# Rotary embedding over sixteen batches: the first store is issued by GpSimd instead of ScalarE

## The chip, the cores and the metric

The kernel runs on one core of one Trainium2 chip. A core has five instruction streams: TensorE (matmuls), VectorE (DVE), ScalarE (ACT), GpSimd (POOL) and SyncE (SP). Each stream executes in order, and waits on semaphores that the others and the DMAs raise. Data moves between the chip's main memory (DRAM) and the core's on-chip memory by DMA; sixteen DMA engines do the moving, and a DMA is put to them by an instruction on SyncE, ScalarE or GpSimd. Each of these issuers has a queue of its own. The metric is the device time of one execution, in microseconds (us); lower is better.

## The reference: what is computed

The input `x` is 16 batches of 512 positions of 1024 numbers (f32); the 1024 numbers are 16 heads of 64. In each head the first 32 numbers (`x1`) and the last 32 (`x2`) are rotated by an angle that depends on the position alone:

```python
x = x.reshape(batch, seq, num_heads, head_dim)
x1, x2 = x[..., :half_dim], x[..., half_dim:]
rotated = np.concatenate([
    x1 * cos - x2 * sin,
    x1 * sin + x2 * cos
], axis=-1)
```

`cos` and `sin` are 512 by 32. Input and output are 33.55 MB each, so 67.1 MB pass through the DMA engines in every execution.

## The kernel before

**Tiling.** The work is cut into eight slabs. A slab is 128 partitions by 8192 f32 numbers, which is 32 KB in each partition and 4.19 MB in all. An on-chip buffer called `room` has six slots of one slab each (`slots = 6`), and slab s lives in slot s modulo 6. Loading, computing and storing all work in place in the slot.

**Loads** (line 71, on SyncE). Six DMAs bring the eight slabs: slabs 0 and 1 singly, slabs 2 and 3 as one DMA of 8.39 MB, slabs 4 and 5 as one of 8.39 MB, and slabs 6 and 7 singly (the dictionary `loads`). The first four are issued at the start. Slab 6 goes into the slot of slab 0, so its load may be issued only once the store of slab 0 has landed; slab 7 waits in the same way for the store of slab 1.

**Compute.** A slab of the middle of the kernel is one pass; slabs 0, 6 and 7 are two passes of half a slab each. A pass has five instructions:

- ScalarE casts the f32 data to bf16 in place (line 144, "the cast");
- VectorE multiplies twice with the cos and sin tables (line 165) and adds (line 168), all in bf16;
- ScalarE writes the result back as f32 over the slot (line 170, "the widening").

The tables themselves are built once at the start, by GpSimd, TensorE and VectorE (lines 79 to 133).

**Stores** (line 174, on ScalarE). Seven DMAs: slabs 0, 1, 2 and 3 singly, slabs 4 and 5 together (8.39 MB), slabs 6 and 7 singly. Because they are issued by ScalarE, a store's instruction stands in the same in-order stream as the casts and widenings.

**What sets the order.** The source is a plain loop over the passes, but the framework under it reorders the instructions of each engine with its own estimates of durations, and so the order on ScalarE is not exactly that of the source. In the kernel before, the order on ScalarE around the first stores is: cast of slab 0 (two halves), cast of slab 1, widening of slab 0 (two halves), store of slab 0, cast of slab 2, widening of slab 1, cast of slab 3, store of slab 1, widening of slab 2, cast of slab 4, store of slab 2, widening of slab 3, cast of slab 5, store of slab 3, widening of slab 4, first cast of slab 6, widening of slab 5, second cast of slab 6, store of slabs 4 and 5. A store's issue starts about 0.1 us after the instruction ahead of it has started, if the widening that it needs is done.

The functions that the change touches:

Of the kernel before, what the change touches and what calls it, by code (L numbers as in the profile page):

```python
# [2 lines left out]

# [4 lines left out]


@with_exitstack  # L10
def kernel(
    ctx: ExitStack,
    tc: tile.TileContext,
    x: bass.AP,
    cos: bass.AP,
    sin: bass.AP,
    num_heads: int,
    out: bass.AP,
):
    nc = tc.nc  # L20
    P = nc.NUM_PARTITIONS

    batch, seq, dim = x.shape
    nh = num_heads
    hd = dim // nh
    half = hd // 2
    bf16 = mybir.dt.bfloat16
    f32 = mybir.dt.float32

    nb = 2  # L30
    slots = 6
    nslabs = batch // nb
    G = 2
    rpp = nb * seq // P
    W = rpp * dim
    SP = seq // rpp
    TW = rpp * half

    out_flat = out.rearrange("b s h d -> b s (h d)")

    singles = ctx.enter_context(tc.tile_pool(name="singles", bufs=1))
    psum = ctx.enter_context(tc.tile_pool(
        name="psum", bufs=1, space=bass.MemoryType.PSUM))


    def dram(t, s, k):
        return bass.AP(tensor=t.tensor,
                       offset=t.offset + s // G * (G * nb * seq * dim) + s % G * W,
                       ap=[[G * W, P], [1, k * W]])


    def view(t, offset, *dims):
        return dataclasses.replace(t, offset=t.offset + offset,
                                   ap=[t.ap[0], *[list(d) for d in dims]])


    room = singles.tile([P, slots * W], f32, tag="room")
    halves = room.bitcast(bf16)


    def slab(s, k):
        return view(room, s % slots * W, (1, k * W))


    loads = {0: 1, 1: 1, 2: 2, 4: 2, 6: 1, 7: 1}
    stores = {0: 1, 1: 1, 2: 1, 3: 1, 4: 2, 6: 1, 7: 1}


    def load(s):
        k = loads[s]  # L70
        nc.sync.dma_start(out=slab(s, k), in_=dram(x, s, k))  # L71

    TR = 32
    TQ = seq // TR // rpp
    TC = seq * half // TR
    raw = singles.tile([P, TC], f32, tag="raw")
    nc.vector.memset(raw, 0.0)  # L79


    def load_tables(queue):
        for i, src in enumerate((cos, sin)):
            to = dataclasses.replace(
                raw, offset=raw.offset + i * raw.ap[0][0],
                ap=[[P // TR * raw.ap[0][0], TR], [1, TC]])
            queue.dma_start(out=to, in_=bass.AP(
                tensor=src.tensor, offset=src.offset, ap=[[TC, TR], [1, TC]]))


    load(0)
    load_tables(nc.scalar)
    for s in loads:
        if 0 < s < slots:
            load(s)

    GP = SP // G
    GT = G // TQ  # L100
    pick = singles.tile([P, 3 * GT * P], bf16, tag="pick")
    nc.gpsimd.memset(pick, 0.0)  # L102


    def selection(g, h):
        return pick[:, (g * GT + h // TQ) * P:(g * GT + h // TQ + 1) * P]


    for g in range(3):
        for h in range(0, G, TQ):  # L110
            part = view(selection(g, h), 0, (GP, P // GP), (1, GP))
            nc.gpsimd.affine_select(  # L112
                out=part, in_=part, compare_op=mybir.AluOpType.not_equal,
                fill=-1.0 if g == 2 else 1.0,
                base=-(1 if g else 0) - h // TQ * (P // TR),
                pattern=[[0, P // GP], [-(G // TQ) * (P // TR), GP]],
                channel_multiplier=1)

    raw_b = singles.tile([P, TC], bf16, tag="raw_b")
    nc.gpsimd.tensor_copy(out=raw_b, in_=raw)  # L120

    tab = {}


    def table(h):
        acc = psum.tile([P, 2 * rpp * hd], f32, tag=f"acc{h}")
        for g, at in ((0, 0), (0, half), (2, rpp * hd), (1, rpp * hd + half)):
            nc.tensor.matmul(  # L128
                view(acc, at, (hd, rpp), (1, half)), selection(g, h),
                view(raw_b, h % TQ * TW, (half, rpp), (1, half)),  # L130
                start=True, stop=True)
        tab[h] = singles.tile([P, 2 * rpp * hd], bf16, tag=f"tab{h}", name="tab")
        nc.vector.tensor_copy(out=tab[h], in_=acc)  # L133

    def span(u):
        s, r, n = u
        at, m = s % slots * W + r * dim, n * dim
        return (m, view(room, at, (1, m)), view(halves, 2 * at, (1, m)),
                view(halves, 2 * at + m, (1, m)))


    def cast(u):
        m, full, low, high = span(u)
        nc.scalar.copy(out=low, in_=full)  # L144

    passes = []
    for s in range(nslabs):  # L150
        n = rpp if 1 <= s < nslabs - 2 else rpp // 2
        passes += [(s, r, n) for r in range(0, rpp, n)]


    cast(passes[0])
    for i, u in enumerate(passes):
        s, r, n = u
        if s < G and r == 0:
            table(s)
        if i + 1 < len(passes):  # L160
            cast(passes[i + 1])
        m, full, low, high = span(u)
        turned = view(low, half, (hd, n * nh), (-half, 2), (1, half))
        for out_, in_, a in ((high, turned, rpp * hd), (low, low, 0)):
            nc.vector.tensor_mul(  # L165
                out=out_, in0=in_,
                in1=view(tab[s % G], a + r * hd, (hd, n), (0, nh), (1, hd)))
        nc.vector.tensor_add(out=high, in0=low, in1=high)  # L168

        nc.scalar.copy(out=full, in_=high)  # L170
        if r + n == rpp:
            for t, k in stores.items():
                if t + k - 1 == s:
                    nc.scalar.dma_start(out=dram(out_flat, t, k), in_=slab(t, k))  # L174
                    for v in range(t + slots, t + k + slots):
                        if v in loads:
                            load(v)


# [1 line left out]
_INS = ['x', 'cos', 'sin', 'num_heads']  # L181
_OUTS = [((16, 512, 16, 64), 'float32')]

_NUMBERS = {'num_heads': 16}


# [26 lines left out]
```

## Time and profile before

| what | us |
|---|---|
| median of 3 runs | 162.26 (162.25 to 162.39) |
| the profiled execution's own time | 162.28 |
| its span in the profile | 160.5 |
| VectorE busy | 109.9 (68% of the span) |
| ScalarE busy | 113.3 (71%) |
| GpSimd busy | 2.1 (1%) |
| share of 16 DMA engines' span, both queues together | 98.0% |

In the profile, instructions are named by engine and by line of the kernel (L144 is the cast). `ACTq`, `SPq` and `POOLq` are the issuing sides of ScalarE, SyncE and GpSimd. A DMA's issue takes some tenths of a microsecond; the time from there until the data have landed is given apart. `q1` is SyncE's DMA queue and `q10` is ScalarE's (the loads and the stores, told apart by their bytes). A packet of the DMA is one row of one partition: 32,768 bytes for a DMA of one slab, 65,536 for a DMA of two.

### The profile page before, as it was taken

The numbers are of one execution on the slowest core, as the hardware profiler recorded it, in microseconds if no ns is written. First come the engines' busy times: TensorE is split into PE (matmuls) and PEld (weight loads), VectorE is DVE, ScalarE is ACT, GpSimd is POOL, SyncE is SP. The second block draws the span as 40 slices with busy tenths as digits, with TensorE's granted clock in tenths as the row PEclk, the third lists the DMA queues.
The fourth block names the chain that finished last, engine by engine and source line by source line (L and its number), as shares of the span: only waits on it lengthen the run. The fifth ranks groups of instructions, "written<-read, shape, count | busy, mean of one in ns | idle before, by whom it ended". The sixth has DMA issues, their size and how long they took to land.

```text
span 160.5 us, 162 instructions
## 1 busy us (share of the span) xinstructions
PE 1.9 (1%) x8; PEld 1.1 (1%) x8; DVE 109.9 (68%) x36; ACT 113.3 (71%) x23; POOL 2.1 (1%) x9
## 2 busy tenths in 40 slices
PE   0004000000000000000000000000000000000000
PEld 0002000000000000000000000000000000000000
DVE  1002999999900999899789989999649999800000
ACT  3006939991089999997999999929999999170000
POOL 3001000000000000000000000000000000000000
DMA  7999999969599999999999999999996996999994
GB/s 261 408 408 392 523 392 523 506 278 523 245 408 392 555 490 392 392 392 392 465 441 400 433 474 400 433 474 400 408 604 294 523 490 294 400 474 433 392 474 180
DMA packets 1968, 67.24 MB, mean 419 GB/s; under 512 B 240, under 2 KB 240, under 8 KB 304
## 3 DMA queue, kind: packets, MB, share of 16 engines
q1 hardware_dynamic: 864, 33.55, 49.4%
q10 hardware_dynamic: 1104, 33.69, 48.6%
HBM read 33.69 MB, written 33.55 MB: 419 GB/s over the span
## 4 chain that ended last, share of the span: by engine, by line
ACT 36%; DMA 27%; DVE 13%; issue 12%; another core or an unknown queue 1%; SPq 0%; ACTq 0%
DMA room<-in_x_dram 27%; ACT room L170 22%; ACT room L144 14%; DVE room L165 8%; DVE room L168 4%; SPq L71 0%; ACTq L174 0%; ACTq L170 0%
## 5 line engine op out<-in xcount | busy, mean ns | idle before, releaser
L165 DVE TENSOR_TENSOR room<-room,tab 128x4096 bf16<-128x4096 bf16 (+1 forms) x22 | 71.6, 3259 | 15.0 <-ACT room L144 14.6
L144 ACT CAST room<-room 128x4096 bf16<-128x4096 f32 (+1 forms) x11 | 56.6, 5153 | 20.9 <-DMA room<-in_x_dram 20.9
L170 ACT CAST room<-room 128x4096 f32<-128x4096 bf16 (+1 forms) x11 | 56.6, 5154 | 6.6 <-DVE room L168 6.6
L168 DVE TENSOR_TENSOR room<-room 128x4096 bf16<-128x4096 bf16 (+1 forms) x11 | 35.9, 3261 | 0.3
L133 DVE CAST tab<-acc 128x1024 bf16<-128x1024 f32 x2 | 2.4, 1219 | 13.6 <-PE acc L128 13.6
L144 ACT ACT_TABLE_LOAD x1 | 1.3, 1283 | 2.7 <-issue 2.7
L128 PE MATMUL acc<-raw_b,pick 128*128 128x256 bf16 x8 | 1.9, 415 | 13.9 <-POOL raw_b L120 13.9
L128 PEld LDWEIGHTS <-pick 128*128 128x128 bf16 x8 | 1.1, 140 | 14.2 <-issue 12.2
L79 DVE MEMSET raw<- 128x512 f32 x1 | 0.5, 485 | 0.9 <-PEq L194 0.9
L112 POOL TENSOR_SCALAR_AFFINE_SELECT pick<-pick 128x128 bf16<-128x128 bf16 x3 | 0.8, 309 | 0.1
L120 POOL CAST raw_b<-raw 128x512 bf16<-128x512 f32 x1 | 0.6, 610 | 11.2 <-DMA raw<-in_sin_dram 11.2
L102 POOL MEMSET pick<- 128x384 bf16 x1 | 0.4, 418 | 0.3 <-POOLq L194 0.3
L194 POOL MEMSET const-float32-0.0<- 128x1 f32 x1 | 0.1, 98 | 0.2 <-issue 0.2
L194 POOL MEMSET const-bfloat16-1.0<- 128x1 bf16 x1 | 0.1, 101 | 0.0
L194 POOL MEMSET const-uint8-127<- 128x1 uint8 x1 | 0.1, 101 | 0.0
L194 POOL MEMSET const-float32-1.0<- 128x1 f32 x1 | 0.1, 98 | 0.0
## 6 DMA issues: line engine op xcount, KB each, us to landing
out_dram<-room ACTq DMA_DIRECT2D x6, 4096.0 KB, 32.5
room<-in_x_dram SPq DMA_DIRECT2D x4, 4096.0 KB, 22.3
raw<-in_cos_dram ACTq DMA_DIRECT2D x1, 64.0 KB, 7.9
raw<-in_sin_dram ACTq DMA_DIRECT2D x1, 64.0 KB, 11.1
room<-in_x_dram SPq DMA_DIRECT2D x2, 57.5
out_dram<-room ACTq DMA_DIRECT2D x1, 25.1
```

Source lines behind the costliest of these rows:

```text
L79: nc.vector.memset(raw, 0.0)
L102: nc.gpsimd.memset(pick, 0.0)
L112: nc.gpsimd.affine_select(out=part, in_=part, compare_op=mybir.AluOpType.not_equal, fill=-1.0 if g == 2 else 1.0, base=-(1 if g else 0) - ...
L120: nc.gpsimd.tensor_copy(out=raw_b, in_=raw)
L128: nc.tensor.matmul(view(acc, at, (hd, rpp), (1, half)), selection(g, h), view(raw_b, h % TQ * TW, (half, rpp), (1, half)), start=True, sto ...
L133: nc.vector.tensor_copy(out=tab[h], in_=acc)
L144: nc.scalar.copy(out=low, in_=full)
L165: nc.vector.tensor_mul(out=out_, in0=in_, in1=view(tab[s % G], a + r * hd, (hd, n), (0, nh), (1, hd)))
L168: nc.vector.tensor_add(out=high, in0=low, in1=high)
L170: nc.scalar.copy(out=full, in_=high)
L194: nc = _bacc.Bacc("TRN2", target_bir_lowering=False, num_devices=1)
```

## The change

[...]

```diff
         if r + n == rpp:
             for t, k in stores.items():
                 if t + k - 1 == s:
-                    nc.scalar.dma_start(out=dram(out_flat, t, k), in_=slab(t, k))
+                    queue = nc.scalar if t else nc.gpsimd
+                    queue.dma_start(out=dram(out_flat, t, k), in_=slab(t, k))
```

The built program differs in more than this one instruction, because the framework orders ScalarE's stream anew. The start of it, from the widening of slab 0 on (line 174 of before is line 175 of after):

```
before                         after
widening slab 0 (two halves)   widening slab 0 (two halves)
store slab 0                   widening slab 1
cast slab 2                    cast slab 2
widening slab 1                store slab 1
cast slab 3                    cast slab 3
store slab 1                   widening slab 2
widening slab 2                cast slab 4
cast slab 4                    store slab 2
...                            ...
```

From the widening of slab 2 on, the two orders are the same. On GpSimd the new store is the last instruction of the stream; it waits for the widening of slab 0's second half. VectorE's order and SyncE's order of instructions do not change; the load of slab 6 waits for GpSimd's store of slab 0, and the load of slab 7 for ScalarE's store of slab 1.

## The prediction

> **What bounds the kernel now.** I read the page's busy line first and the DMA lines under it, then DMA by stretches, then the order in time with the waits.
>
> ```profile
> PE 1.9 (1%) x8; PEld 1.1 (1%) x8; DVE 109.9 (68%) x36; ACT 113.3 (71%) x23; POOL 2.1 (1%) x9
> DMA packets 1968, 67.24 MB, mean 419 GB/s; under 512 B 240, under 2 KB 240, under 8 KB 304
> q1 hardware_dynamic: 864, 33.55, 49.4%
> q10 hardware_dynamic: 1104, 33.69, 48.6%
> ```
>
> No compute engine is over 71% busy; the DMA engines are taken for 98.0% of the span. 67.24 MB at the 434 GB/s that the undisturbed stretches move are 155 us of the 160.5. So little can be gained: the first packets' delay, the last landing, and one dip below. Much can be lost, if the DMA engines are ever left without work.
>
> The DMA view between 46 and 68 us, and between 36 and 44 us, when the first store starts:
>
> ```profile
> DMA packets 192, 9.44 MB, mean 429 GB/s; under 512 B 0, under 2 KB 0, under 8 KB 0
> q1 hardware_dynamic: 96, 6.29, 65.9%
> q10 hardware_dynamic: 96, 3.15, 33.1%
> ...
> DMA packets 66, 2.92 MB, mean 365 GB/s; under 512 B 9, under 2 KB 9, under 8 KB 9
> ```
>
> Between 46 and 68, loads (q1) and store 0 (q10) have equal numbers of packets, 96 and 96: the queues take turns. A load packet of 64 KB takes 2.42 us on its engine, a store packet of 32 KB 1.21, so a round is 3.63 us. Between 36 and 44, (429 - 365) / 429 of 8 us is lost: a dip of 1.2 us, in which the packet that runs as the first store starts takes 3.6 to 3.9 us instead of 2.42 (single packets are read from the trace).
>
> Order in time:
>
> ```profile
> 36.93 0.35 ACTq L174 DMA_DIRECT2D out_dram<-room  x1
> 39.62 4.42 DVE L168 TENSOR_TENSOR room<-room 128x8192 bf16<-128x8192 bf16 x1
> 44.91 7.02 ACT L144 CAST room<-room 128x8192 bf16<-128x8192 f32 x1 [8.02 <-DMA room<-in_x_dram]
> 51.84 7.01 ACT L170 CAST room<-room 128x8192 f32<-128x8192 bf16 x1
> 51.96 8.89 DVE L165 TENSOR_TENSOR room<-room,tab 128x8192 bf16<-128x8192 bf16 x2 [7.92 <-ACT room L144]
> 58.88 0.34 ACTq L174 DMA_DIRECT2D out_dram<-room  x1
> 65.68 7.01 ACT L170 CAST room<-room 128x8192 f32<-128x8192 bf16 x1
> 73.80 7.02 ACT L144 CAST room<-room 128x8192 bf16<-128x8192 f32 x1 [1.11 <-DMA room<-in_x_dram]
> 115.17 0.34 ACTq L174 DMA_DIRECT2D out_dram<-room  x1
> ...
> SPq L71 <- DMA out_dram<-room: 87.4, 2, 67.3
> ```
>
> ScalarE stands idle from 36.9 to 44.9 for slabs 2 and 3, and slab 1's widening, whose sum is ready at 39.62 + 4.42 = 44.04, stands behind that cast. Slab 4's cast waits for its load until 73.8. The last line is SyncE holding the loads of slabs 6 and 7 for stores 0 and 1.
>
> DMA issued from ScalarE in 87-89, 114-116, 128-131 and 142-145, with the time to landing:
>
> ```profile
> out_dram<-room ACTq DMA_DIRECT2D x1, 4096.0 KB, 33.2
> ...
> out_dram<-room ACTq DMA_DIRECT2D x1, 25.1
> ...
> out_dram<-room ACTq DMA_DIRECT2D x1, 4096.0 KB, 20.6
> ...
> out_dram<-room ACTq DMA_DIRECT2D x1, 4096.0 KB, 16.1
> ```
>
> Issue plus landing: store 3 lands at 87.77 + 33.2 = 120.95, stores 4/5 at 140.3, 6 at 150.0, 7 at 159.6. The steps, 19.3, 9.7 and 9.7, are exactly the bytes at 434 GB/s, so at the end each store queues behind the one before. The cover of compute over DMA is smallest at stores 4/5: issued at 115.17, while store 3 lands at 120.95. If that issue slips by more than the cover, DMA stands still and the end moves.
>
> **The change, part by part.** The sum is made against the profiled execution: span 160.5, time 162.28, 1.8 around it, against a median of 162.26.
>
> *Issue taken from ScalarE (0.35 us).* It falls in ScalarE's idle 8 us: worth nothing. Without that cover it would be 0.35.
>
> *Issue added on GpSimd.* GpSimd's stream is empty after its table cast at 13.9 us and nothing is queued behind the store: no cost there. [...]
>
> *ScalarE's new order.* Widening of slab 1 now starts at 44.06, and the cast of slab 2 one pitch of a full slab later (51.84 - 44.91 = 6.93), at 51.0 instead of 44.91. Store 1 is issued at 51.1 instead of 58.88. Cast of slab 3 at 57.9. VectorE does slab 2 in 13.34 us (51.96 to 65.30 before), now 58.0 to 71.35; the widening of slab 2 starts at 71.4 (before 65.68), and the cast of slab 4 can start at 78.35 instead of 73.80. This 4.55 us is certain if the order is kept.
>
> *The third queue.* Store 0 has GpSimd's queue, store 1 comes into ScalarE's at 51.1 and no longer stands behind it. If the queues still take turns, a round is 2.42 + 1.21 + 1.21. Load 4/5 has 8.39 MB / 16 / 65,536 = 8 packets on each engine, of which 6 start after 52; in 5 to 6 of those rounds store 1 adds a packet of 1.21, 6.1 to 7.3 us. Load 4/5, landed at 73.78 before, lands at 79.9 to 81.1, and that, not 78.35, starts the cast of slab 4. Stores 0 to 2 and loads 6 and 7 gain or lose nothing by it: the same bytes in another order. Store 0 lands near 73, load 6 after 23.7 us as before is there before its cast is due (it started at 101.49 before, 27.7 after that of slab 4).
>
> *The end.* From the cast of slab 4 to the issue of stores 4/5 is 115.17 - 73.80 = 41.4 us in either order; now 121.3 to 122.5. The DMA engines run out of work where store 3 landed, 120.95, since the bytes ahead are the same. What a start on idle engines costs, the first load bounds: 12.6 us to landing less 9.7 of transfer is 2.9; the tables' packets take 0.3 of it, and the very first packets, at 1.9 instead of 1.2, 0.7. I take 1.9, between 1.6 (the first packet 1.0 after the first issue, the last landing 0.6 after its packet) and 2.9. The end moves by (cast of slab 4) + 41.4 + 1.9 - 120.95, that is by that cast's start less 77.65: 2.25 to 3.45, middle 2.85. Stores 6 and 7, issued 55.5 and 69.7 after the cast, come before the DMA needs them.
>
> *The dip.* 1.2 us, gone or kept: no row shows a GpSimd store. I keep it, since the next queue's first store may pay it as well.
>
> Sum: 0 + 0 + 2.85 = 2.85; 162.28 + 2.85 = 165.1.
>
> **Rivals.**
>
> *A: turns longer or shorter than a row.* The rows show one row per turn for the two queues there are. If GpSimd's queue gave its 8 rows per engine in one turn, that is 9.7 us in which loads 2/3 cannot end: from 44.9 to about 53.4, the cast of slab 2 at 53.4 instead of 51.0, slab 4's at 80.8 to 82.5: 3.2 to 4.85 more, 166.3. [...] With turns much smaller than a row, store 0 gets its bytes mostly after load 4/5 (about 70) and shares with store 1 or 2 from there: 4.19 MB at 217 GB/s, landing near 90 to 92. Load 6, 20.6 to 23.7 later at 113, holds the cast in front of slab 5's widening; stores 4/5 go out at 113 + 3.5 + 6.9 = 123.4, plus 4.4: 166.7.
>
> *B: store 0 starts late.* VectorE works from 35.16 to 44.04 without a gap. If GpSimd's descriptors had to wait for it, store 0 would start 7 us late, one or two of its packets would fall behind load 4/5, and slab 4's cast would be at 78.35 to 79.9: 0.7 to 2.25, about 163.8. [...] No run here shows it.
>
> *C, the other side: the dip goes.* If GpSimd's start does not disturb the running packet, 1.2 us come back at 40 us and everything behind moves up with it. It ends faster only if load 4/5 is in by 78.35 as well, with at most three packets of store 1 ahead of its end (73.78 - 1.2 + 3 x 1.21 = 76.2): 0.7 - 1.2 = -0.5, 161.8, at best 161.1 if the start on idle engines were nothing to pay. For it: the dip is there once, at a first store of ScalarE. Against: store 1 has 20 us beside load 4/5. With the dip gone and the turns as forecast it is 163.9.
>
> **How the numbers follow.** Forecast 0.45 (165.1, its own range 164.5 to 165.7). A 0.20 (166.3 to 166.7). B 0.12 (163.8). C with late loads 0.09 (163.9). C with loads in time 0.14 (161.1 to 162.3). Within 0.2%, some 0.3 us, is what a measurement here cannot tell from no change: the edges of B and C make 0.08; faster 0.12; slower 0.80. The range leaves out most of C's fast end and the worst of A: 161.9 to 167.0.
>
> **What would show it.** Right: store 1 issued at 51, cast of slab 2 at 51, cast of slab 4 at 80 to 81 with a wait for DMA, stores 4/5 issued near 122, a hole in the DMA there, three queues with packets between 53 and 73. Wrong: slab 4's cast at 78.4 with no wait; store 0 landing near 50 or 90; loads 2/3 late; no dip at 40 us; or a hole elsewhere.

## The result, and the profile after

The changed kernel takes 164.38 us (median of 5 runs, 164.0 to 165.18) where the kernel before takes 162.25 (now of 5 runs as well, 162.06 to 162.39): 1.0133 times as long, with a 95% interval of 1.012 to 1.0147. Forecast were 165.1 us, slower with a chance of 0.80, and a range of 161.9 to 167.0. The profiled execution took 164.26, with a span of 162.5 against 160.5.

The page of the changed kernel, the DMA line, the line of each queue (packets, MB, share of 16 engines' span) and the group of the new store:

```profile
DMA packets 1968, 67.24 MB, mean 414 GB/s; under 512 B 240, under 2 KB 240, under 8 KB 304
q1 hardware_dynamic: 864, 33.55, 48.9%
q10 hardware_dynamic: 960, 29.49, 42.1%
q0 software_dynamic: 144, 4.19, 6.0%
L175 POOL DMA_DIRECT2D out_dram<-room x1 | 0.7, 690 | 23.3 <-ACT room L170 23.3
```

The bytes and packets are the same; the 4.19 MB of store 0, issued by GpSimd, are in a third queue, `q0`. The profile gives its kind as software_dynamic, that of the other two as hardware_dynamic; it is called the software ring below, and what stands behind the name no run shows. Share by share, 97.0% of the DMA engines' time is taken instead of 98.0%, in a longer span: 1% of 160 us have become idle, and the packets' own time is unchanged. So the loss is DMA engines without work, and the question is only where.

The changed kernel in order of time, the lines that answer to those shown of before:

```profile
37.20 0.69 POOL L175 DMA_DIRECT2D out_dram<-room  x1 [23.32 <-ACT room L170]
39.63 4.43 DVE L168 TENSOR_TENSOR room<-room 128x8192 bf16<-128x8192 bf16 x1
44.15 7.02 ACT L170 CAST room<-room 128x8192 f32<-128x8192 bf16 x1 [7.24 <-DVE room L168]
51.07 7.01 ACT L144 CAST room<-room 128x8192 bf16<-128x8192 f32 x1
51.19 0.35 ACTq L175 DMA_DIRECT2D out_dram<-room  x1
71.55 7.02 ACT L170 CAST room<-room 128x8192 f32<-128x8192 bf16 x1 [6.54 <-DVE room L168]
79.94 7.02 ACT L144 CAST room<-room 128x8192 bf16<-128x8192 f32 x1 [1.37 <-DMA room<-in_x_dram]
121.31 0.34 ACTq L175 DMA_DIRECT2D out_dram<-room  x1
```

Slab 1's widening now runs from 44.15, before the cast of slab 2, which slips from 44.91 to 51.07. Store 1 goes out at 51.19 instead of 58.88. The widening of slab 2 starts at 71.55 and ends at 78.6, and then ScalarE waits 1.37 for load 4/5: its cast of slab 4 starts at 79.94 instead of 73.80, and everything behind it on ScalarE is 6.1 late, up to the issue of stores 4/5 at 121.31 instead of 115.17.

The DMA view of the changed kernel between 54 and 70 us, the queues' lines:

```profile
q1 hardware_dynamic: 48, 3.15, 45.4%
q10 hardware_dynamic: 64, 2.10, 30.3%
q0 software_dynamic: 48, 1.57, 22.8%
```

These are the turns of three queues: three load packets (2.42 us each on its engine), three of store 0 and four of store 1 (1.21 each) on every engine, the fourth by where the cut falls. Loads had 65.9% of the DMA engines while store 0 alone stood beside them; now they have 45.4%, and load 4/5 lands at 79.92 instead of 73.78.

In the single packets, every engine moves one row of the load, one of store 1 and one of store 0 by turns, from 55 to 71 us.

The stretches of the changed kernel around the issue of stores 4/5 (us, then busy time and count of PE, PEld, DVE, ACT and POOL, clock, DMA share and GB/s; a packet counts whole where it starts):

```profile
119.00:120.00 1.00, 0.00 (x0) 0.00 (x0) 1.00 (x1) 1.00 (x1) 0.00 (x0) 1.00 0.76 328
120.00:121.00 1.00, 0.00 (x0) 0.00 (x0) 1.00 (x1) 1.00 (x1) 0.00 (x0) 1.00 0.01 0
121.00:122.00 1.00, 0.00 (x0) 0.00 (x0) 0.03 (x1) 1.00 (x2) 0.00 (x0) 1.00 0.00 0
122.00:123.00 1.00, 0.00 (x0) 0.00 (x0) 0.00 (x0) 1.00 (x1) 0.00 (x0) 1.00 2.46 1049
```

No packet of a row starts between 120 and 122 (the 0.01 is packets of 4 bytes). Store 3's last packets, of 1.21 us, end at 120.0 to 120.6 and the first of stores 4/5 start at 122.1 to 122.3: each engine stands still for 1.6 to 2.3 us, 1.9 on average. In the kernel before, all sixteen engines have started on stores 4/5 by 120.6, without a gap behind store 3. Its stretches from 120 to 122:

```profile
120.00:121.00 1.00, 0.00 (x0) 0.00 (x0) 0.97 (x1) 1.00 (x1) 0.00 (x0) 1.00 2.12 918
121.00:122.00 1.00, 0.00 (x0) 0.00 (x0) 0.99 (x1) 1.00 (x1) 0.00 (x0) 1.00 0.00 0
```

The zero in its second row is no idle time: the packets that started between 120 and 121 take 2.42 us each.

The landing of the four last DMAs of ScalarE in the changed kernel, cut out as the four were for the kernel before:

```profile
out_dram<-room ACTq DMA_DIRECT2D x1, 4096.0 KB, 27.1
...
out_dram<-room ACTq DMA_DIRECT2D x1, 20.8
...
out_dram<-room ACTq DMA_DIRECT2D x1, 4096.0 KB, 16.3
...
out_dram<-room ACTq DMA_DIRECT2D x1, 4096.0 KB, 11.8
```

Store 3 lands at 93.91 + 27.1 = 121.0, as before (120.95). Stores 4/5 land at 121.31 + 20.8 = 142.1, which is 1.8 later than before, store 6 at 151.8 and store 7 at 161.5, 1.9 later than before. Up to 120 us nothing is lost, and behind 122 next to nothing more: the program ends 1.0 us after the last landing, where it was 0.9 in the kernel before.

### The profile page after: what moved, and what is told of

Read it like the earlier page. It is cut to its first block, busy times and chain, and to the rows that moved or that the text cites. A ratio compares the mean times of both kernels' runs of the same rounds, so it can differ in the third digit from the quotient of the medians.

```text
span 162.5 us, 166 instructions
## 1 busy us (share of the span) xinstructions
PE 1.9 (1%) x8; PEld 1.1 (1%) x8; DVE 109.8 (68%) x36; ACT 113.3 (70%) x23; POOL 2.7 (2%) x10
## 3 DMA queue, kind: packets, MB, share of 16 engines
q0 software_dynamic: 144, 4.19, 6.0%
## 4 chain that ended last, share of the span: by engine, by line
DVE 37%; ACT 37%; issue 8%; DMA 7%; another core or an unknown queue 1%; PE 1%; ACTq 1%; POOL 0%; POOLq 0%; DVEq 0%
DVE room L165 25%; ACT room L170 24%; ACT room L144 13%; DVE room L168 11%; DMA raw<-in_sin_dram 7%; DVE tab L133 1%; PE acc L128 1%; POOL raw_b L120 0%; ACTq L87 0%; DVE raw L79 0%; ACTq L175 0%; ACTq L170 0%; POOLq L120 0%; DVEq L165 0%
## 5 line engine op out<-in xcount | busy, mean ns | idle before, releaser
L165 DVE TENSOR_TENSOR room<-room,tab 128x4096 bf16<-128x4096 bf16 (+1 forms) x22 | 71.6, 3259 | 21.3 <-ACT room L144 20.8
L175 POOL DMA_DIRECT2D out_dram<-room x1 | 0.7, 690 | 23.3 <-ACT room L170 23.3
## 6 DMA issues: line engine op xcount, KB each, us to landing
out_dram<-room ACTq DMA_DIRECT2D x1, 20.8
```

The costliest lines, as they stand in the source:

```text
L165: nc.vector.tensor_mul(out=out_, in0=in_, in1=view(tab[s % G], a + r * hd, (hd, n), (0, nh), (1, hd)))
L175: queue.dma_start(out=dram(out_flat, t, k), in_=slab(t, k))
```

## The experiments

The forecast's rule, with the idle start as the changed kernel shows it: stores 4/5 are issued 41.4 after the cast of slab 4 starts; on idle DMA engines they land 1.47 later than their transfer of 19.33 takes (142.11 - 121.31 - 19.33); store 3 has landed at 120.95. So the end moves by the start of slab 4's cast less 78.1, and not at all below that. The 1.47 is the changed kernel's own, so the other runs test the rule and the changed kernel does not. Each run is compared with runs of the kernel before on the same chip.

**The order alone.** Store 0 stays with ScalarE; slab 1's widening goes ahead of slab 2's cast.

```diff
-        if i + 1 < len(passes):
+        if i + 1 < len(passes) and s != 1:
             cast(passes[i + 1])
...
-        nc.scalar.copy(out=full, in_=high)
+        wide = nc.scalar.copy(out=full, in_=high)
+        if s == 1:
+            with tc.issue_after(wide.ins):
+                cast(passes[i + 1])
```

> The change's new order on ScalarE without its queue: store 0 stays with ScalarE, issued right behind slab 0's widening as before, and slab 1's widening goes ahead of slab 2's cast as in the changed kernel. Theory (the end moves by the start of slab 4's cast plus 41.4 to the issue of stores 4/5, plus 1.5 to start idle DMA engines, less the 120.95 at which store 3 lands): load 4/5 lands near 73.8 as before, slab 4's cast starts at 78.35 because of the order, stores 4/5 go out at 119.7, the end moves by 0.2, time 162.3 to 162.6. Rival, the order alone costs all of it: 164.2 to 164.5. Rival, the software ring costs all of it: 162.25, and no sign of an order's effect.

Measured: 162.65 against 162.31, ratio 1.0021 (1.0011 to 1.003); that is 0.05 above the theory's range. In its order of time the cast of slab 4 stands without a wait for DMA:

```profile
78.36 7.01 ACT L144 CAST room<-room 128x8192 bf16<-128x8192 f32 x1
```

Load 4/5 landed at 73.81 and store 1, though issued at 51.08, behind store 0 at 90.7, as in the kernel before. The rule gives 78.36 - 78.1 = 0.26 for the 0.34 measured. The order alone is one sixth of the loss.

**The queue alone.** Store 0 is issued by GpSimd; ScalarE's order is held to that of before.

```diff
-            cast(passes[i + 1])
+            nxt = cast(passes[i + 1])
...
-        nc.scalar.copy(out=full, in_=high)
+        if s == 1:
+            with tc.issue_after(nxt.ins):
+                nc.scalar.copy(out=full, in_=high)
+        else:
+            nc.scalar.copy(out=full, in_=high)
```

> The change's queue without its new order: store 0 is issued by GpSimd, and ScalarE's order is held to that of before (slab 2's cast ahead of slab 1's widening), so store 1 goes out at 58.9. Theory: three queues take turns only from 59 on, load 4/5 lands at 77.4 to 78.8 instead of 79.9, slab 4's cast starts there, stores 4/5 go out at 118.8 to 120.2, just inside or just outside the cover: time 162.2 to 162.9. Rival, the software ring itself is what costs: 164.2 to 164.5. Rival, only the order matters: 162.25.

Measured: 162.41 against 162.31, ratio 1.0004 (0.9995 to 1.0014): no change that can be measured. Yet the third queue does its work on load 4/5, which lands at 77.52, and on the cast that waits for it:

```profile
77.54 7.02 ACT L144 CAST room<-room 128x8192 bf16<-128x8192 f32 x1 [4.78 <-DMA room<-in_x_dram]
```

ScalarE waits 4.78 instead of 1.11, and it costs nothing, because 77.54 is still under 78.1. So the software ring as such is not the cost. The two parts alone come to 0.44 us; together they cost 2.1. Both draw on the same cover, but they do not simply add. Here load 4/5 lands three packets of 1.21 us later than before; in the changed kernel it is five, because the new order also issues store 1 at 51.19 instead of 58.95, and so store 1 stands beside the load for longer. ScalarE is free for slab 4's cast at 78.57 in the changed kernel, and it is the load that holds the cast until 79.94.

**Store 1 in the software ring too.** ScalarE's order is written out as in the changed kernel, so that no third queue arises beside load 4/5; VectorE's order is left to the framework.

```diff
-        queue = nc.scalar if t else nc.gpsimd
+        queue = nc.scalar if t > 1 else nc.gpsimd
```

> The changed kernel with store 1 moved to GpSimd as well, behind store 0 in the same software ring; ScalarE's order is written out and is that of the changed kernel. Theory: there is no third queue beside the loads while load 4/5 is under way, so load 4/5 lands near 73.8, slab 4's cast starts at 78.35, the end moves by 0.2: 162.3 to 162.7, though twice the bytes go through the software ring. Rival, each store in the software ring costs by itself: 166 or more. Rival, the loss is that of the order: 164.4.

Measured: 167.12 against 162.31, ratio 1.0294 (1.0279 to 1.031). The number is one that the first rival allows (166 or more), and far from the theory's. But load 4/5 landed at 73.62, as the theory says, and the cast of slab 4 was at 82.77 all the same. The order of time shows why: the framework had given VectorE one of slab 3's multiplications ahead of slab 2's addition.

```profile
58.19 13.22 DVE L186 TENSOR_TENSOR room<-room,tab 128x8192 bf16<-128x8192 bf16 x3 [14.06 <-ACT room L144]
71.33 4.42 DVE L189 TENSOR_TENSOR room<-room 128x8192 bf16<-128x8192 bf16 x1
75.84 7.02 ACT L190 CAST room<-room 128x8192 f32<-128x8192 bf16 x1 [10.76 <-DVE room L189]
```

Slab 2's addition starts at 71.33, its widening at 75.84 instead of 71.55. Three multiplications stand in the row where the changed kernel has two. The rule gives 82.77 - 78.1 = 4.7; measured 4.8.

**The same with VectorE's order written out.**

```diff
+            with tc.issue_after(added) if s > 1 else nullcontext():
                 nc.vector.tensor_mul(
...
-        nc.vector.tensor_add(out=high, in0=low, in1=high)
+        added = nc.vector.tensor_add(out=high, in0=low, in1=high).ins
```

> The run with stores 0 and 1 both in the software ring, once more, with VectorE's order written out as well: there, VectorE had been given a multiplication of slab 3 ahead of the addition of slab 2, which put slab 4's cast at 82.8. Theory: load 4/5 lands near 73.7 again, slab 4's cast starts at 78.4, stores 4/5 go out at 119.8, the end moves by 0.2 to 0.4 and the time is 162.4 to 162.8. Rival, two stores in the software ring cost more than one: 165 to 167 with slab 4's cast at 78.4.

Measured: 162.97 against 162.28, ratio 1.0068 (1.0034 to 1.0103); the medians alone are 0.4% apart. The median is 0.2 above the theory's range. Of ten executions seven took 162.8 to 163.0, and three 164.7 to 165.9. The seven are far from 165 to 167, so the run before it does not speak for a fixed price of the ring; the three are near it, and what made them long was not found. Load 4/5 landed at 73.72, and slab 4's cast:

```profile
78.52 7.01 ACT L144 CAST room<-room 128x8192 bf16<-128x8192 f32 x1
```

The rule gives 0.4 for 0.7 between the medians, with twice the changed kernel's bytes in the software ring and a third of its loss. In the profiled execution, one of the seven, the last store lands 0.46 later than in the kernel before (160.08 against 159.62), as the rule has it. Another 0.2 lies behind that landing: the program ends 1.07 us after it, instead of 0.89. This stretch at the end is 0.9 to 1.0 in the three runs with one store in the ring, 1.06 to 1.07 in the two with two, and 0.8 to 0.9 in those with none.

**The late cast without GpSimd.** The kernel before, with ScalarE's order written out, all stores with ScalarE, and n small copies in front of slab 4's cast (5 and 13).

```diff
+        if i == 3:
+            for _ in range(n):
+                act(lambda: nc.scalar.copy(out=dump, in_=raw))
         if ahead:
             act(cast, passes[ahead[0]])
```

> The kernel before (ScalarE's order written out, the same as there; all stores with ScalarE) with five small copies on ScalarE, into a scratch tile that nobody reads, put in front of slab 4's cast; nothing is taken away from the computation. Slab 4's cast is then at about 76, 2 later than before. Theory: the end moves by that cast's start less 78.1, and by nothing below that: 162.2 to 162.5. Rival, the end follows every delay of that cast: 164.3.

> As the run with five copies, but with thirteen: slab 4's cast at about 81. Theory: the end moves by that cast's start less 78.1, that is 2.5 to 3.2, and stands in a hole of the DMA at 121 to 124: 164.8 to 165.5, with no GpSimd store and no third queue. Rival, the late cast alone does nothing and the loss needs the software ring or the early store 1: 162.3.

Measured: with five, 162.30 against 162.28, ratio 1.0000 (0.9991 to 1.0009); with thirteen, 165.13 against 162.28, ratio 1.0178 (1.0163 to 1.0193). The casts, with five and with thirteen:

```profile
75.82 7.01 ACT L144 CAST room<-room 128x8192 bf16<-128x8192 f32 x1
```

```profile
80.95 7.01 ACT L144 CAST room<-room 128x8192 bf16<-128x8192 f32 x1
```

The stretches of the run with thirteen, columns as above:

```profile
120.00:121.00 1.00, 0.00 (x0) 0.00 (x0) 1.00 (x1) 1.00 (x1) 0.00 (x0) 1.00 0.01 0
121.00:122.00 1.00, 0.00 (x0) 0.00 (x0) 1.00 (x1) 1.00 (x1) 0.00 (x0) 1.00 0.00 0
122.00:123.00 1.00, 0.00 (x0) 0.00 (x0) 0.03 (x1) 1.00 (x2) 0.00 (x0) 1.00 0.00 0
```

The first 2.0 us of delay (75.82 - 73.80) cost nothing; 7.15 cost 2.85, which is 80.95 - 78.1 to the second digit, and the hole is there, one row longer than in the changed kernel. The hole needs neither the software ring nor an early store 1: it needs slab 4's cast to be late.

**The hole filled.** The changed kernel with the double store cut in two.

```diff
-    stores = {0: 1, 1: 1, 2: 1, 3: 1, 4: 2, 6: 1, 7: 1}
+    stores = {0: 1, 1: 1, 2: 1, 3: 1, 4: 1, 5: 1, 6: 1, 7: 1}
```

> The changed kernel with the double store of slabs 4 and 5 cut into two, so that slab 4 can go out at 107.7, long before store 3 has landed. Slab 4's cast still starts near 79.9. Theory: the hole in the DMA near 121 is gone, and the next place where the cover is too small decides, store 7: issued at 149.7, plus 1.5, plus 9.7 of transfer, is 160.8 against 159.6 before, so 1.2 is left of 2.0: time 163.3 to 163.6. Rival, the loss is spread over the run and not in that hole: 164.4. Rival, the hole is all there is: 162.3.

Measured: 163.31 against 162.31, ratio 1.0060 (1.0045 to 1.0075). Store 4 goes out at 107.70, and packets run on through 121. Store 7 goes out at 149.56, and there the new gap is:

```profile
148.00:149.00 1.00, 0.00 (x0) 0.00 (x0) 0.00 (x0) 1.00 (x1) 0.00 (x0) 1.00 0.68 295
149.00:150.00 1.00, 0.00 (x0) 0.00 (x0) 0.00 (x0) 0.54 (x1) 0.00 (x0) 1.00 0.01 0
150.00:151.00 1.00, 0.00 (x0) 0.00 (x0) 0.00 (x0) 0.00 (x0) 0.00 (x0) 1.00 1.22 524
```

Half of the loss came back and half moved to the next place with too little cover, as forecast.

**The dip at 40 us.** The kernel before with a store of 64 KB at the start.

```diff
+    warm = singles.tile([P, 128], f32, tag="warm")
+    nc.vector.memset(warm, 0.0)
     load(0)
+    last = dram(out_flat, nslabs - 1, 1)
+    nc.scalar.dma_start(out=dataclasses.replace(last, ap=[last.ap[0], [1, 128]]), in_=warm)
     load_tables(nc.scalar)
```

> The kernel before with one small store of 64 KB ahead of the tables' loads, of zeros into a part of the output that slab 7's store overwrites at the end; it is there for the dip of 1.2 that the DMA shows at 39 to 43 when the first store starts, in the kernel before as in the changed one. If the dip is what the first store of an execution pays, whoever issues it, it moves to the start, where it may lie beside the first packets' own delay: 161.0 to 162.3, with no long packet at 39. If it belongs to the end of load 2/3 or to the first store of full size, it stays at 39 and the time is 162.2 to 162.6.

Measured: 162.13 against 162.28, ratio 0.9991 (0.9981 to 1.0): the same within what can be told. With the small store ahead of the tables' loads, store 0 went out at 44.41 instead of 36.93. The DMA view of this run, between 36 and 44 us and between 43 and 51 us:

```profile
DMA packets 64, 3.15 MB, mean 393 GB/s; under 512 B 16, under 2 KB 16, under 8 KB 16
```

```profile
DMA packets 48, 2.62 MB, mean 328 GB/s; under 512 B 0, under 2 KB 0, under 8 KB 0
```

In the single packets, the long one has left 39 us, where 2.43 now stands for it, and has gone with store 0 to 46.5, where it is 3.4 to 3.5. So the dip belongs neither to the end of load 2/3 nor to the first store of any size; it comes with the first store of full size. The time does not show this: 162.13 lies in the range that was expected if the dip went to the start, and just under the 162.2 to 162.6 of the other case. That store 0 could go out 7.5 later without a loss shows that its start is not what the end of this kernel depends on.

All the runs by one rule:

| run | load 4/5 lands | cast of slab 4 | cast - 78.1, or 0 | time over before |
|---|---|---|---|---|
| before | 73.78 | 73.80 | 0 | 0 |
| five copies | 73.87 | 75.82 | 0 | 0.0 |
| queue alone | 77.52 | 77.54 | 0 | 0.1 |
| order alone | 73.81 | 78.36 | 0.3 | 0.3 |
| both in the ring, VectorE's order held | 73.72 | 78.52 | 0.4 | 0.7 |
| the change | 79.92 | 79.94 | 1.8 | 2.1 |
| thirteen copies | 73.71 | 80.95 | 2.9 | 2.9 |
| both in the ring, VectorE's order left free | 73.62 | 82.77 | 4.7 | 4.8 |

In the single packets of these traces, the engines stand idle behind store 3 for 0.3 us on average with the order alone, 0.6 with both stores in the ring and VectorE's order held, 1.9 in the changed kernel, 3.1 with thirteen copies and 4.9 in the last row, and not at all in the first three: the hole is as long as the rule says, to 0.3 us.

## Why the prediction was right

- **What bounds the kernel, and the cover.** Right. The DMA engines were the bound, the smallest cover was at stores 4/5, and the one hole is there. The run with the double store cut in two and those with copies on ScalarE show that it is this hole; the only other cost that the traces show is the 0.1 us behind the last landing.
- **Issue taken from ScalarE and added on GpSimd: nothing.** Right. GpSimd's issue took 0.69 us, and store 0's first packets ran at 42.6 to 43.2, as in the kernel before (42.5 to 43.2). The issue ran from 37.20 on, and the first packets before 44.0, while VectorE worked from 35.2 to 44.0 with no more than 0.04 us between its instructions: the start 7 us late of rival B did not happen. A hold of a few us would not show here, because the engines were busy with load packets until 42.6.
- **ScalarE's new order.** Right: slab 2's cast at 51.07 (forecast 51.0), its widening at 71.55 (71.4), and the cast of slab 4 free to start at 78.36 in the run with the order alone (78.35).
- **The third queue.** Right: load 4/5 landed at 79.92, forecast 79.9 to 81.1. Five packets of store 1 came ahead of its end, the lower of the two numbers that the forecast had. Store 0 landed at 76.27 and not near 73; load 6 behind it was still in at 99.25, 8.4 before its cast. Rival A did not happen: one row is one turn in the software ring too. In the changed kernel the engines switched after each row from 45 to 73 us, and only the first two rows of store 0 ran one behind the other (from 42.6 and from 43.9 us on, and in the kernel before from 42.5 and from 43.7).
- **The end.** The mechanism is right, the sum 1.0 too large, and the median lies just below the forecast's own range of 164.5 to 165.7. Of that 1.0, 0.56 is the middle between five and six packets, where five came. The rest is the start on idle engines, taken as 1.9 between bounds of 1.6 and 2.9. It measured 1.47 in the changed kernel, and 1.43 to 1.47 in the other five runs with such a start (landing less issue less transfer). The lower bound was made of two parts read at other places, and the real one is below it. With 79.94 and 1.47 the sum is 1.84 instead of 2.85. The profiled executions differ by 1.98, of which 1.88 is the last landing and 0.1 the stretch behind it; the medians differ by 2.13. The executions of the changed kernel scatter by 1.2 us, against 0.3 before, and the profiled one lies below the median.
- **The dip.** Kept, as taken: between 36 and 44 us the changed kernel moves 344 GB/s, the kernel before 365, and the long packets take 3.5 to 4.0 us, in the kernel before 3.3 to 4.0 (the prediction read 3.6 to 3.9). Rival C, the faster side, needed it gone.

What the prediction did not say, and the runs do: neither part of the change costs much by itself, 0.3 us the order and nothing measurable the queue. The order takes 4.6 of the cover at stores 4/5, the third queue alone 3.7; the cover stands at 4.3 (78.1 - 73.8); only together, with 6.1, do they go through it by much.

## What to carry to other kernels

Where the DMA engines are the bound, ask of a change first two things: whether it leaves them without work at some point, and how much cover each later issue has left; in these runs a delay of 2.0 us inside the cover cost nothing and one of 7.15 cost 2.85, and two parts that cost 0.3 us and nothing measurable alone cost 2.1 together, because only together did they go through it by much. Store 0, moved to a queue of its own, took turns row by row with the load and with store 1, and load 4/5 landed 3.7 us later with the queue alone and 6.1 later in the changed kernel, although no byte was added. And read the built order of every engine, also of those that the edit doesn't name: here a change of one issuer reordered ScalarE, and in one experiment VectorE, by more than the edit itself was worth.

## What the hardware showed that was not expected

- The start of a DMA on idle engines costs 1.43 to 1.47 us in six runs, stores of 8.39 MB and of 4.19 MB alike, while the first load of the program landed 2.9 later than its transfer takes.
- On every engine, the load packet just ahead of the first full-size store of an execution was stretched by 0.8 to 1.6 us (3.2 to 4.1 instead of 2.42, read from single packets of all ten traces), whether ScalarE or GpSimd issues the store. A store of 64 KB ahead did not take that away: the packet was 3.4 to 3.5 there. Store 1, the first full-size one in ScalarE's queue in the changed kernel, shows no such packet. What causes it stays open.
- With two stores in the software ring and VectorE's order held, three executions of ten took 1.7 to 3 us longer than the other seven. The four executions of the other run with two stores there lie within 0.2 us, and no run with one store or none scattered so far apart. The cause was not found.
